# Strassen products for the last ten inner tiles of the first FFN of a hybrid block

## The chip, the cores and the metric

The kernel runs on one core of a Trainium2 chip. The metric is the time of one execution on the device in microseconds (us). TensorE (PE) does the matrix products from weights and moving operands in SBUF into PSUM banks, VectorE (DVE) and ScalarE (ACT) the elementwise work, GpSimd (POOL) little; SyncE (SP) and POOL issue most of the transfers.

## The reference

One decoder block in fp32: a macaron of two SwiGLU FFNs round a pair of token mixers. D = 1024, 512 tokens and 16 meta tokens ahead of them (L = 528), inner width D_FF = 2816.

```python
h = concat([meta, x])                                    # 528 x 1024
h = h + 0.5 * swiglu_ffn(rms_norm(h, ffn1_norm), ffn1_w1, ffn1_w3, ffn1_w2)
u = rms_norm(h, mix_norm) @ w_in                         # conv, ssm and gate inputs
h = h + (g_conv * conv_branch(u) + g_ssm * s5_branch(u)) @ w_out
h = h + 0.5 * swiglu_ffn(rms_norm(h, ffn2_norm), ffn2_w1, ffn2_w3, ffn2_w2)
out = rms_norm(h)[:, 16:]

def swiglu_ffn(x, w1, w3, w2):
    return (silu(x @ w1) * (x @ w3)) @ w2
```

The tokens lie along the free axis; a tile of 128 rows holds 128 features. The change is in the first FFN, before which stands only the load of x.

## The kernel before

**Products of fp32.** Every operand is split into a high part, cast to fp32r by ACT (line 120), and a low part, the difference, by DVE (line 121). A product is three matmuls: high by high, weights' low by high, high by low (`mm3`, line 147).

**First FFN, up.** D_FF is 22 inner tiles of 128. For a tile f, `ffn_up` loads the 1024 x 128 pieces of `ffn1_w1` and `ffn1_w3` (each as one 128 x 1024 tile, 512 KB, by SP into `raw`), splits them (`whi`, `wlo`) and multiplies them with x: 8 steps k of the depth, 3 terms, two halves of 264 tokens, each half in a PSUM bank of its own (`two()`). The moving operands `xh[k]`, `xl[k]` (split x with the norm's gain) stay in SBUF. The norm's factor r comes in where DVE evicts the banks (line 217), then ACT takes silu, DVE multiplies (line 239, `take`) and splits the hidden tile.

**First FFN, down.** Tiles go in groups of 8, 7 and 7. Behind a group, `down` multiplies for each of the eight output tiles k all hidden tiles of the group with `ffn1_w2`, and DVE adds the two halves into the residual `h[k]` (line 564). In the last group each output tile is followed by the operand of the next stage and its sum of squares.

**Preparation of the SSM.** `prepare_ssm` is a generator of elementwise work on the SSM's parameters, independent of the tokens: exponentials, the matrices bm, the c matrices (`cm`, line 288, written out to DRAM as `cd`), and the e tables (lines 499 to 514). `prep_step()` runs one step at a lower priority (`LATER`), after tiles with f even or above 8.

**Second FFN.** It does its 512 tokens already by Strassen pairs: `moving` forms four combinations t1 to t4 of the quarters of x, `pair` takes two inner tiles by seven `product`s (line 932) in place of eight, from weight quarters and sums of quarters. A `quarter` with two indices is loaded by SP and the second one added by a DMA of POOL (line 900). Down projections are taken between the products.

**The order.** No order is written out by hand. The program issues operations as above; a scheduler of the tile framework orders each engine by priority, with its own model of when operands are ready. Pools of buffers bound how far ahead work can go: 6 PSUM banks for these products (`psp`), 4 raw tiles (`rawp`), 7 split weights (`wsp`), 4 temporaries (`tp`), 18 hidden tiles (`hid1`).

Of the kernel before, what the change touches and what calls it, by code (L numbers as in the profile page):

```python
# [15 lines left out]
P = 128  # L16
# [10 lines left out]
G = 32  # L27
# [9 lines left out]
TAPS = 500  # L37
MAGIC = float(1.5 * 2 ** 23)
# [3 lines left out]
def tile_hybrid_block(  # L42
    ctx: ExitStack, tc: tile.TileContext,
    xt, cols, lam, bt, ct, dt, ffn1_w1, ffn1_w3, ffn1_w2, w_in, conv_proj, w_v, w_g, w_out,
# [38 lines left out]
    def tmp2(tag="m", bufs=2):  # L83
        return mp.tile([P, L], F32, tag=tag, name=nm(tag), bufs=bufs)
# [5 lines left out]
    mp = tst.enter_context(tc.tile_pool(name="mp", bufs=2, side="right"))  # L90
    ones = mp.tile([P, P], F32, name="ones", bufs=1)
# [119 lines left out]

    def ffn_gate(pss, r, n, take):
# [42 lines left out]
    def prepare_ssm(prep):  # L255
# [228 lines left out]
        while m < C:  # L484
            t = prep.tile([P, 3, G], F32, name=f"turn{m}")
# [10 lines left out]
        for i in range(4):  # L496
# [4 lines left out]
            for j, t in enumerate(turn):  # L501
                m = 2 ** j
                n = min(m, C - m)
                w = prep.tile([P, 2, 8, n], F32, tag="tw", name=nm("tw"))
# [19 lines left out]
    with ExitStack() as st:  # L524
        hid = st.enter_context(tc.tile_pool(name="hid1", bufs=18))
        pst = st.enter_context(ExitStack())
        prep = pst.enter_context(tc.tile_pool(name="prep", bufs=1))
# [25 lines left out]
        ssm_steps = prepare_ssm(prep)  # L553
# [16 lines left out]

        f0 = 0
        for nf in (8, 7, 7):
            hd = Hidden(slot, L)
            for f in range(f0, f0 + nf):
                if f == 0:
                    ffn_gate(first, r, L, hd.take)
                else:
                    ffn_up(ffn1_w1, ffn1_w3, f, r, L, hd.take)
                if f % 2 == 0 or f > 8:
                    prep_step()  # L580
            for k in range(KD):
# [6 lines left out]
        for _ in ssm_steps:  # L588
            raise AssertionError
        pst.close()  # L590


    with ExitStack() as st:
        mx = st.enter_context(tc.tile_pool(name="mx", bufs=1))
        sps = st.enter_context(ExitStack())
# [274 lines left out]
    with ExitStack() as st:  # L870
# [12 lines left out]
        def wide(pool, tag):  # L883
            return pool.tile([P, 8 * P], F32, tag=tag, name=nm(tag))

        def w4(tile_):
            return tile_.rearrange("p (w k c) -> p w k c", w=2, k=4)

        def split_w(src):
            hi = wsp.tile([P, 8 * P], F32R, tag="w", name=nm("whi"))  # L890
            lo = wsp.tile([P, 8 * P], F32R, tag="w", name=nm("wlo"))
            split(hi, lo, src)
            return w4(hi), w4(lo)

        def quarter(p, q, add=None):

            t = wide(rawp, "raw") if add is None else wide(xp, "x")
            nc.sync.dma_start(t, ffn2_up[p, q])
            if add is not None:
                PL.dma_start(t, ffn2_up[p, add], accum_op=ALU.add)  # L900
            return t

# [43 lines left out]
        def pair(p, hd):  # L946

            r11, s1, s3, r12, r22 = (quarter(p, *q) for q in ((0,), (1, 3), (0, 1), (2,), (3,)))
# [37 lines left out]
        def plain(p, hd):  # L986

            for tile_ in range(2):
                pss = [one(), one()]
                for kh in range(2):  # L990
                    wh, wl = split_w(quarter(p, 2 * kh + tile_))
# [86 lines left out]
def layout(i):  # L1078
# [13 lines left out]
    def up(w1, w3):  # L1092
# [18 lines left out]
        "ffn1_w1": tiles(i["ffn1_w1"], P), "ffn1_w3": tiles(i["ffn1_w3"], P),  # L1111
# [28 lines left out]
```

## Time and profile before

| | us |
|---|---|
| median of 3 runs (1074.3 to 1076.5) | 1074.4 |
| the profiled execution | 1074.19 |
| its span, in the trace | 1072.4 |
| TensorE busy | 1058.8 |
| VectorE busy | 752.2 |
| ScalarE busy | 407.3 |
| GpSimd busy | 42.3 |

The profile is of one execution; the granted TensorE clock was 0.997 of full speed over it. In the page's picture of the span PE is busy for nine tenths and more in all slices but the first and the last. The first FFN ends, with the second normalisation, a little after 417 us; the second one starts its pairs at about 743 us.

### The profile page before, as it was taken

Reading aid. Unit: us, or ns where it says so; the run is one execution under the profiler, and the core shown is the slowest. Engines: PE = TensorE matmul, PEld = TensorE weight load, DVE = VectorE, ACT = ScalarE, POOL = GpSimd, SP = SyncE. Lnnn points to the kernel's source line nnn. Section 1 sums busy time; section 2 is a strip of 40 time slices with the busy share of each in tenths; the row PEclk is TensorE's granted clock in tenths of the full one; section 3 lists DMA queues with packets and bytes.
Section 4 is the critical chain, followed back from the end, with each engine's and each line's share of the span. In section 5 each row is a group of like instructions: output and inputs, shape, how many; then the busy total and the mean of one; then the engine's idle time right before and its main releaser. Section 6 shows DMA issues by size and latency. Waiting matters only on the chain.

```text
span 1072.4 us, 18043 instructions
## 1 busy us (share of the span) xinstructions
PE 1058.8 (99%) x7316; PEld 986.7 (92%) x7316; DVE 752.2 (70%) x1401; ACT 407.3 (38%) x528; POOL 42.3 (4%) x81
## 2 busy tenths in 40 slices
PE   8999999999999999999999999999999999999997
PEld 7999999999999999998888788888999999998896
DVE  7997397953334465889899668558967786686672
ACT  6223322322222243215555363446443343243333
POOL 0000000000000000001000000010000000000001
PEclk9999999999999999999999999999999999999999
DMA  7324364232232232465653223254664464655122
GB/s 248 117 96 104 129 184 173 94 102 91 99 99 79 82 98 98 120 189 153 183 157 119 79 79 118 97 173 112 184 172 126 133 180 128 182 153 153 59 79 79
DMA packets 63267, 136.74 MB, mean 128 GB/s; under 512 B 22352, under 2 KB 29008, under 8 KB 63184
## 3 DMA queue, kind: packets, MB, share of 16 engines
q1 hardware_dynamic: 54192, 111.79, 32.7%
q0 software_dynamic: 4800, 16.78, 7.6%
q10 hardware_dynamic: 4192, 7.02, 2.1%
q8 instruction: 57, 0.93, 0.3%
q14 instruction: 26, 0.21, 0.1%
HBM read 124.50 MB, written 11.01 MB: 126 GB/s over the span
## 4 chain that ended last, share of the span: by engine, by line
PE 96%; DVE 1%; DMA 1%; ACT 1%; issue 0%; POOLq 0%; POOL 0%; SPq 0%; DVEq 0%; ACTq 0%
PE pp L147 62%; PE pp L932 17%; PE pm L1010 9%; PE pp L995 2%; PE pp L1064 2%; PE pm L455 1%; PE pm L649 1%; PE pm L684 1%; PE pm L685 1%; DMA raw<-in_ffn_w_dram 0%; DVE wlo L121 0%; DMA raw<-in_ffn_rows_dram 0%; PE pm L180 0%; DMA h<-in_x_dram 0%; PE pm L193 0%; DVE tl L121 0%
## 5 line engine op out<-in xcount | busy, mean ns | idle before, releaser
L121 DVE TENSOR_TENSOR wlo<-raw,whi 128x1024 fp32r<-128x1024 f32 (+2 forms) x177 | 207.5, 1174 | 185.4 <-issue 98.0
L120 ACT CAST whi<-raw 128x1024 fp32r<-128x1024 f32 (+2 forms) x177 | 178.2, 1011 | 396.7 <-PE pp L147 269.3
L147 PE MATMUL pp<-xh,whi 128*128 128x264 f32 (+1 forms) x1024 | 236.3, 301 | 1.6 <-DVE t L217 1.5
L147 PE MATMUL pp<-xl,whi 128*128 128x264 f32 (+1 forms) x1024 | 235.1, 301 | 2.6 <-DVE xl L154 2.6
L147 PE MATMUL pp<-xh,wlo 128*128 128x264 f32 (+1 forms) x1024 | 236.8, 301 | 0.0
L147 PEld LDWEIGHTS pp<-xh,whi 128*128 128x128 f32 x1024 | 165.0, 189 | 8.6 <-issue 1.5
L147 PEld LDWEIGHTS pp<-xl,whi 128*128 128x128 f32 x1024 | 163.6, 189 | 8.7 <-DVE xl L154 2.8
L147 PEld LDWEIGHTS pp<-xh,wlo 128*128 128x128 f32 x1024 | 164.5, 189 | 5.8
L147 PE MATMUL pp<-hd,whi 128*128 128x264 f32 x704 | 116.3, 285 | 0.0
L147 PEld LDWEIGHTS pp<-hd,whi 128*128 128x128 f32 x704 | 98.0, 189 | 0.0
L1010 PE MATMUL pm<-hd,whi 128*128 128x512 f32 x288 | 94.9, 395 | 0.0
L932 PE MATMUL pp<-th,whi 128*128 128x256 f32 x320 | 89.7, 282 | 0.8 <-ACT th L120 0.8
L932 PE MATMUL pp<-th,wlo 128*128 128x256 f32 x320 | 90.0, 282 | 0.2 <-DVE wlo L121 0.2
L932 PE MATMUL pp<-tl,whi 128*128 128x256 f32 x320 | 89.6, 282 | 0.3 <-DVE tl L121 0.3
L726 DVE SCALAR_TENSOR_TENSOR acc<-z,col,acc 128x512 f32<-128x512 f32 x120 | 84.8, 745 | 1.8 <-ACT acc L724 1.4
L147 PE MATMUL pp<-hd,wlo 128*128 128x264 f32 x352 | 72.6, 286 | 0.0
L932 PE MATMUL pp<-xh,whi 128*128 128x256 f32 x240 | 67.4, 281 | 0.0
L932 PE MATMUL pp<-xl,whi 128*128 128x256 f32 x240 | 67.3, 281 | 0.0
L932 PE MATMUL pp<-xh,wlo 128*128 128x256 f32 x240 | 67.3, 280 | 0.0
L1010 PEld LDWEIGHTS pm<-hd,whi 128*128 128x128 f32 x288 | 54.1, 188 | 11.3
L932 PEld LDWEIGHTS pp<-th,whi 128*128 128x128 f32 x320 | 60.1, 188 | 2.0 <-ACT th L120 1.0
L932 PEld LDWEIGHTS pp<-th,wlo 128*128 128x128 f32 x320 | 60.2, 188 | 1.4 <-DVE wlo L121 0.4
(279 smaller groups left out, 1619.2 us busy)
## 6 DMA issues: line engine op xcount, KB each, us to landing
raw<-in_ffn_w_dram SPq DMA_DIRECT2D x50, 512.0 KB, 3.5
raw<-in_ffn_up_dram SPq DMA_DIRECT2D x34, 512.0 KB, 4.4
raw<-in_w_in_dram SPq DMA_DIRECT2D x28, 512.0 KB, 3.6
x<-in_ffn_up_dram SPq DMA_DIRECT2D x20, 512.0 KB, 3.9
x<-in_ffn_up_dram POOLq DMA_DIRECT2D x20, 512.0 KB, 7.2
rd<-in_ffn_w_dram SPq DMA_DIRECT2D x24, 384.0 KB, 4.0
raw<-in_ffn_w_dram SPq DMA_DIRECT2D x16, 448.0 KB, 3.2
raw<-in_w_out_dram SPq DMA_DIRECT2D x8, 512.0 KB, 3.6
```

The lines of the kernel that those rows point to most:

```text
L120: A.copy(hi, src)
L121: V.tensor_tensor(lo, src, hi.bitcast(F32), op=ALU.subtract)
L147: nc.tensor.matmul(o, a[:, k, off:off + P], mov(k, n, lo), start=(k == 0 and j == 0), stop=(k == nk - 1 and j == 2))
L455: nc.tensor.matmul(ps[:, g, :], xm[(g0 + g) // Q][:, (g0 + g) % Q].rearrange("p l h -> p (l h)"), t[:, g, :], start=True, stop=True)
L649: nc.tensor.matmul(pb[j][:, g * C:(g + 1) * C], bm[:, g * P:(g + 1) * P], ub[i][:, j * 4 + g, :], start=True, stop=True)
L684: nc.tensor.matmul(o, tm[:, gs_], ub[i][:, j * 4 + g, CM:], start=True, stop=False)
L685: nc.tensor.matmul(o, cm[:, gs_], sa[i][:, j * 4 + g, CM:C], start=False, stop=True)
L726: V.scalar_tensor_tensor(o, src, w, o, op0=ALU.mult, op1=ALU.add)
L932: nc.tensor.matmul(ps[:, i * N2:(i + 1) * N2], a[:, i, k], b(k, lo), start=(first and i == 0 and k == 0 and j == 0), stop=(i == 1 and k == ...
L995: nc.tensor.matmul(pss[i], a[:, i, k], x[k + 4 * kh][:, :S], start=(kh == 0 and k == 0 and j == 0), stop=(kh == 1 and k == 3 and j == 2))
L1010: nc.tensor.matmul(ps, a[:, q * P:(q + 1) * P], hd.hl[q][lo], start=(q == 0 and j == 0), stop=(q == nf - 1 and j == 2))
L1064: nc.tensor.matmul(ps, a[:, tk], wts[q][b][j], start=False, stop=(q == nf - 1 and jj == 2))
```

## The change

`NP1 = 12`: inner tiles 0 to 11 are computed as before, in groups of 6 and 6. Tiles 12 to 21 become five pairs by Strassen products, in groups of 4 and 6 tiles, whose weights come packed by quarters (`ffn1_up`). A pair works on the two halves of 264 tokens; every product has two results (`w1` and `w3`) and takes two PSUM banks (`two()`).

- `moving(k)` stands after every second down projection of the second group. It loads x again, scales it, forms t1 to t4 and splits them; t1 takes the place of the second half of `xh[k]`, `xl[k]` for k below 4, and t2 to t4 get tiles of their own.
- The down projections of the group of 4 are taken one after each of the seven products of the next group's first pair and the eighth after the first product of its second pair; those of the last group stand at the end.
- The steps of the preparation come after tiles 0, 2, 4 (two), 6, 7 and 8 and after the first down projection. Its pool is closed after tile 11, and its room goes to `sp1`, the buffers of the pairs. The pool `turns` (powers for the e tables) moves to the other side, and the mixers' temporaries `m` get a pool that opens after the FFN.
- `hid1` has 14 tiles in place of 18. `wide`, `w4`, `split_w` and `quarter` move out of the second FFN, unchanged but for their buffers.

```diff
+NP1 = 12
...
-        hid = st.enter_context(tc.tile_pool(name="hid1", bufs=18))
+        hid = st.enter_context(tc.tile_pool(name="hid1", bufs=14))
...
+        def again(k):
+            raw = rawp.tile([P, 8 * P], F32, tag="raw", name=nm("raw"))[:, :L]
+            nc.sync.dma_start(raw, xt[k * P:(k + 1) * P, :])
+            t = tmp()
+            A.activation(t, raw, AF.Copy, scale=g1[:, k:k + 1])
+            return t
+
+        def moving(k):
+            xa, xb = again(k), again(k + 4)
+            t = sp1.tile([P, 4, HALF], F32, tag=f"c{k % 2}", name=nm("c"))
+            V.tensor_tensor(t[:, 0], xa[:, i1], xa[:, i0], op=ALU.subtract)
+            V.tensor_tensor(t[:, 1], xb[:, i1], t[:, 0], op=ALU.subtract)
+            V.tensor_tensor(t[:, 2], xa[:, i1], xb[:, i1], op=ALU.subtract)
+            V.tensor_tensor(t[:, 3], xb[:, i0], t[:, 1], op=ALU.subtract)
+            split(xh[k][:, i1], xl[k][:, i1], t[:, 0])
+            tw = [sp1.tile([P, 3, HALF], F32R, name=f"tw{q}{k}") for q in "hl"]
+            split(*tw, t[:, 1:])
+            tws.append(tw)
...
+        def product(pss, w, name, first=True):
+            b = b_of(name)
+            for i, ps in enumerate(pss):
+                for k in range(4):
+                    for j, (a, lo) in enumerate(((w[0], 0), (w[1], 0), (w[0], 1))):
+                        nc.tensor.matmul(ps, a[:, i, k], b(k, lo),
+                                         start=(first and k == 0 and j == 0),
+                                         stop=(k == 3 and j == 2), skip_group_check=not first)
+
+        def pair(p, hd):
+            r11, s1, s3, r12, r22 = (quarter(ffn1_up, sp1, p, *q)
+                                     for q in ((0,), (1, 3), (0, 1), (2,), (3,)))
+            ca, cb = (sp1.tile([P, 2, L], F32, tag=f"c{q}", name=nm("c")) for q in range(2))
+            t1, t2 = v2h(tmp()), v2h(tmp())
...
+            b1 = two()
+            product(b1, split_w(r11), "11")
+            for i in range(2):
+                A.copy(t1[:, i], b1[i])
+            yield
+            V.tensor_tensor(r11, r11, s1, op=ALU.add)
+            b6 = two()
+            product(b6, split_w(r11), "t2")
+            each(t1, b6, t1, ALU.subtract)
+            yield
+            b5 = two()
+            product(b5, split_w(s1), "t1")
+            each(t2, b5, t1, ALU.add)
+            yield
+            b7 = two()
+            product(b7, split_w(s3), "t3")
+            each(cb[:, :, i1], b7, t2, ALU.add)
+            yield
+            product(b1, split_w(r12), "21", first=False)
+            each(ca[:, :, i0], b1, r[:, i0], ALU.mult)
+            V.tensor_tensor(r12, r12, r11, op=ALU.add)
+            yield
+            b3 = two()
+            product(b3, split_w(r12), "22")
+            each(ca[:, :, i1], b3, t2, ALU.subtract)
...
+            product(b7, split_w(r22), "t4", first=False)
+            each(cb[:, :, i0], b7, t1, ALU.add)
...
-        for nf in (8, 7, 7):
+        for nf in (6, 6):
...
-                if f % 2 == 0 or f > 8:
+                if f in (0, 2, 4, 6, 7, 8):
                     prep_step()
+                if f == 4:
+                    prep_step()
...
             for k in range(KD):
                 down(f0, nf, hd, k)
-                if f0 + nf == NF:
-                    operand(k, hv[k], g2[:, k:k + 1], L)
-                    ssn.add(hv[k], V)
+                if f0 == 0 and k == 0:
+                    prep_step()
+                if f0 and k % 2:
+                    moving(k // 2)
             f0 += nf
+        hd = None
+        for nf in (4, 6):
+            old, hd = hd, Hidden(slot, L)
+            todo = [] if old is None else [(f0 - 4, 4, old, k) for k in range(KD)]
+            for p in range((f0 - NP1) // 2, (f0 + nf - NP1) // 2):
+                for _ in pair(p, hd):
+                    if todo:
+                        down(*todo.pop(0))
+            f0 += nf
+        for k in range(KD):
+            down(f0 - 6, 6, hd, k)
+            operand(k, hv[k], g2[:, k:k + 1], L)
+            ssn.add(hv[k], V)
```

DVE in a tile of the third group before: `wlo` is a split weight, `pp` a PSUM bank, `t` the evicted results, `hd` a hidden tile.

```order
621 L121 TENSOR_TENSOR wlo_392_3936<-raw_390_3934,whi_391_3935 128x1024
622 L217 TENSOR_TENSOR t_381_3866<-pp_374_3760,r_24_337 128x264
623 L217 TENSOR_TENSOR t_381_3866<-pp_375_3761,r_24_337 128x264
624 L121 TENSOR_TENSOR wlo_401_4004<-raw_399_4002,whi_400_4003 128x1024
625 L217 TENSOR_TENSOR t_382_3867<-pp_379_3816,r_24_337 128x264
626 L217 TENSOR_TENSOR t_382_3867<-pp_380_3817,r_24_337 128x264
627 L239 TENSOR_TENSOR t_382_3867<-t_382_3867,t_381_3866 128x528
628 L121 TENSOR_TENSOR hd_384_3875<-t_382_3867,hd_383_3874 128x528
```

DVE in the first pair of the changed kernel, from its second product's split on; line 650 evicts, line 672 adds quarters, `x` is a quarter with another added by POOL's DMA.

```order
612 L124 TENSOR_TENSOR wlo_359_3314<-x_337_3203,whi_358_3313 128x1024
613 L650 TENSOR_TENSOR t_342_3212<-pp_348_3247,t_342_3212 128x264
614 L124 TENSOR_TENSOR wlo_361_3344<-raw_338_3206,whi_360_3343 128x1024
615 L650 TENSOR_TENSOR t_342_3212<-pp_349_3248,t_342_3212 128x264
616 L672 TENSOR_TENSOR raw_338_3206<-raw_338_3206,raw_335_3198 128x1024
617 L650 TENSOR_TENSOR t_343_3213<-pp_352_3279,t_342_3212 128x264
618 L650 TENSOR_TENSOR t_343_3213<-pp_353_3280,t_342_3212 128x264
619 L124 TENSOR_TENSOR wlo_365_3377<-raw_338_3206,whi_364_3376 128x1024
620 L650 TENSOR_TENSOR c_341_3211<-pp_356_3311,t_343_3213 128x264
621 L124 TENSOR_TENSOR wlo_369_3414<-raw_339_3208,whi_368_3413 128x1024
622 L650 TENSOR_TENSOR c_341_3211<-pp_357_3312,t_343_3213 128x264
623 L650 TENSOR_TENSOR c_340_3210<-pp_344_3214,r_24_340 128x264
```

Where a split stood once to two evictions that follow each other, splits and evictions now alternate, and an addition of quarters stands ahead of the two evictions of the third product.

DVE before, round the first e table (`e0`), which stands among the down projections of the first group, behind the last c matrix `cm3`.

```order
402 L564 SCALAR_TENSOR_TENSOR h6_104<-pp_184_1967,h6_104 128x264
403 L288 TENSOR_TENSOR cm0_2201<-bt1_795,bt2_796 128x8x16
404 L564 SCALAR_TENSOR_TENSOR h6_104<-pp_185_1968,h6_104 128x264
405 L288 TENSOR_TENSOR cm1_2202<-bt1_795,bt2_796 128x8x16
406 L288 TENSOR_TENSOR cm2_2203<-bt1_795,bt2_796 128x8x16
407 L288 TENSOR_TENSOR cm3_2204<-bt1_795,bt2_796 128x8x16
408 L499 MEMSET e0_2414 128x8
409 L500 MEMSET e0_2414 128x8
410 L121 TENSOR_TENSOR wlo_207_2259<-raw_205_2257,whi_206_2258 128x1024
411 L564 SCALAR_TENSOR_TENSOR h7_105<-pp_189_2025,h7_105 128x264
```

The same place in the changed kernel; line 241 evicts a tile's result, line 263 is its gate product.

```order
396 L312 TENSOR_TENSOR cm2_1416<-bt1_798,bt2_799 128x8x16
397 L312 TENSOR_TENSOR cm3_1417<-bt1_798,bt2_799 128x8x16
398 L124 TENSOR_TENSOR wlo_221_2255<-raw_219_2253,whi_220_2254 128x1024
399 L241 TENSOR_TENSOR t_174_1905<-pp_171_1854,r_24_340 128x264
400 L241 TENSOR_TENSOR t_174_1905<-pp_172_1855,r_24_340 128x264
401 L523 MEMSET e0_1949 128x8
402 L524 MEMSET e0_1949 128x8
403 L263 TENSOR_TENSOR t_174_1905<-t_174_1905,t_173_1904 128x528
404 L534 TENSOR_TENSOR tw_177_1952<-e0_1949,turn1_1916 128x8
405 L535 TENSOR_TENSOR tw_177_1952<-e0_1949,turn1_1916 128x8
```

The first e table now stands among the tiles of the second group, ahead of a gate product.

## Rows read from the trace of the kernel before

**Rows 1.** The page, part 1: busy us of each engine, share, instructions.

```profile
PE 1058.8 (99%) x7316; PEld 986.7 (92%) x7316; DVE 752.2 (70%) x1401; ACT 407.3 (38%) x528; POOL 42.3 (4%) x81
```

**Rows 2.** The page, part 4: the chain that ended last, by engine and by line.

```profile
PE 96%; DVE 1%; DMA 1%; ACT 1%; issue 0%; POOLq 0%; POOL 0%; SPq 0%; DVEq 0%; ACTq 0%
PE pp L147 62%; PE pp L932 17%; PE pm L1010 9%; PE pp L995 2%; PE pp L1064 2%; PE pm L455 1%; PE pm L649 1%; PE pm L684 1%; PE pm L685 1%; DMA raw<-in_ffn_w_dram 0%; DVE wlo L121 0%; DMA raw<-in_ffn_rows_dram 0%; PE pm L180 0%; DMA h<-in_x_dram 0%; PE pm L193 0%; DVE tl L121 0%
```

**Rows 3.** The chain in order of time: start us, us, what.

```profile
135.65 281.36 PE pp L147 x2304
...
743.03 36.06 PE pp L932 x302
```

**Rows 4.** Waits of PE: line, waited for: us in total, times, longest.

```profile
PE pp L147 <- DVE xl L154: 2.6, 1, 2.6
...
PE pp L932 <- ACT th L120: 0.8, 1, 0.8
...
PE pp L932 <- DVE tl L121: 0.3, 1, 0.3
PE pp L932 <- DVE wlo L121: 0.2, 1, 0.2
```

**Rows 5.** Stretches: us, busy PE, PEld, DVE, ACT, POOL (instructions), PEclk, DMA, GB/s.

```profile
165.00:232.00 67.00, 67.00 (x549) 67.00 (x549) 55.03 (x194) 18.64 (x23) 2.02 (x5) 1.00 0.36 117
...
764.00:784.00 20.00, 20.00 (x159) 19.46 (x158) 18.15 (x23) 9.29 (x12) 1.73 (x2) 1.00 0.71 201
...
940.00:966.00 26.00, 26.00 (x219) 25.91 (x218) 23.30 (x27) 12.82 (x17) 1.74 (x2) 1.00 0.59 158
```

**Rows 6.** Groups by shape: count, busy us, mean ns, idle time before.

```profile
L121 DVE TENSOR_TENSOR wlo<-raw,whi 128x1024 fp32r<-128x1024 f32 x153 | 186.7, 1223 | 142.4 <-issue 69.5 <-PE pp L147 50.8 <-PE pp L932 10.5
L120 ACT CAST whi<-raw 128x1024 fp32r<-128x1024 f32 x153 | 160.0, 1050 | 344.2 <-PE pp L147 225.5 <-PE pm L1010 27.4 <-DVE raw L955 26.0
L217 DVE TENSOR_TENSOR t<-pp,r 128x264 f32<-128x264 f32 x88 | 33.9, 424 | 0.1
L121 DVE TENSOR_TENSOR wlo<-rd,whi 128x768 fp32r<-128x768 f32 x24 | 23.0, 957 | 17.3 <-issue 13.8 <-PE pp L932 3.5
L239 DVE TENSOR_TENSOR t<-t,t 128x528 f32<-128x528 f32 x22 | 15.5, 704 | 1.2
L981 DVE TENSOR_TENSOR c<-c,r 128x1024 f32<-128x1024 f32 x10 | 12.2, 1218 | 0.0
```

**Rows 7.** DVE in time: start, us, what; x2 is two back to back.

```profile
749.02 2.35 DVE L121 TENSOR_TENSOR wlo<-raw,whi 128x1024 fp32r<-128x1024 f32 x2
...
253.50 0.77 DVE L564 SCALAR_TENSOR_TENSOR h<-pp,h 128x264 f32<-128x264 f32 x2
...
81.85 0.69 DVE L121 TENSOR_TENSOR hd<-t,hd 128x528 fp32r<-128x528 f32 x1
82.47 0.48 DVE L288 TENSOR_TENSOR xm<-bt,bt 128x128 f32<-128x128 f32 x2
```

**Rows 8.** Loads of weight quarters; POOL's issues in ns; landing of the accumulating ones.

```profile
x<-in_ffn_up_dram SPq DMA_DIRECT2D x20, 512.0 KB, 3.9
...
L900 POOL DMA_DIRECT2D x<-in_ffn_up_dram x20: 863/872/942, 714.1 to 985.3; - x20
...
DMA to landing us min/median/max: 5.2/7.2/8.6
```

**Rows 9.** DVE groups from 137 to 232 us, as in rows 6.

```profile
L513 DVE TENSOR_TENSOR e<-e,turn 128x16 f32<-128x16 f32 (+5 forms) x56 | 10.4, 230 | 0.0
...
L511 DVE TENSOR_TENSOR tw<-e,turn 128x16 f32<-128x16 f32 (+5 forms) x28 | 6.4, 228 | 0.0
L288 DVE TENSOR_TENSOR cm<-bt,bt 128x128 f32<-128x128 f32 x28 | 6.3, 284 | 0.2
...
L288 DVE TENSOR_TENSOR bt<-s_ai,q 128x512 f32<-128x512 f32 x6 | 4.1, 689 | 0.1
```

**Rows 10.** DVE in time, as in rows 7, at the first e table.

```profile
165.51 0.07 DVE L499 MEMSET e<- 128x8 f32 x1 [4.78 <-DMA cd<-cm]
```

More of the change, by code (lines that the diff above doesn't have):

```diff
@@ L83, in tmp2 @@
     def tmp2(tag="m", bufs=2):
-        return mp.tile([P, L], F32, tag=tag, name=nm(tag), bufs=bufs)
+        pool = mmp[0] if tag == "m" else mp
+        return pool.tile([P, L], F32, tag=tag, name=nm(tag), bufs=bufs)
     ident = cst.tile([P, P], F32, name="ident")
@@ L209, in movx, with wide, w4, split_w @@
         return (xl if lo else xh)[k].rearrange("p (t c) -> p t c", t=T)[:, :, CM:]
+    def wide(pool, tag):
+        return pool.tile([P, 8 * P], F32, tag=tag, name=nm(tag))
+    def w4(tile_):
+        return tile_.rearrange("p (w k c) -> p w k c", w=2, k=4)
+    def split_w(src):
+        hi = wsp.tile([P, 8 * P], F32R, tag="w", name=nm("whi"))
+        lo = wsp.tile([P, 8 * P], F32R, tag="w", name=nm("wlo"))
+        split(hi, lo, src)
+        return w4(hi), w4(lo)
+    def quarter(up, xp, p, q, add=None):
+        t = wide(rawp, "raw") if add is None else \
+            xp.tile([P, 8 * P], F32, tag="x", name=nm("x"), bufs=2)
+        nc.sync.dma_start(t, up[p, q])
+        if add is not None:
+            PL.dma_start(t, up[p, add], accum_op=ALU.add)
+        return t
     def ffn_gate(pss, r, n, take):
@@ L484, in prepare_ssm @@
         while m < C:
-            t = prep.tile([P, 3, G], F32, name=f"turn{m}")
+            t = turns.tile([P, 3, G], F32, name=f"turn{m}")
             if not turn:
@@ new lines, in pair, with each @@
+        def pair(p, hd):
[3 more added lines that the diff above has]
+            t1, t2 = v2h(tmp()), v2h(tmp())
+            def each(o, a, b, op):
+                for i in range(2):
+                    V.tensor_tensor(o[:, i], a[i], b[:, i] if len(b.shape) == 3 else b, op=op)
+            b1 = two()
+            product(b1, split_w(r11), "11")
+            for i in range(2):
+                A.copy(t1[:, i], b1[i])
[20 more added lines that the diff above has]
+            each(ca[:, :, i1], b3, t2, ALU.subtract)
+            V.tensor_tensor(ca[:, :, i1], ca[:, :, i1],
+                            r[:, i1].unsqueeze(1).to_broadcast([P, 2, HALF]), op=ALU.mult)
+            A.activation(ca[:, 0], ca[:, 0], AF.Silu)
+            hd.take(ca[:, 1], ca[:, 0])
+            yield
+            product(b7, split_w(r22), "t4", first=False)
+            each(cb[:, :, i0], b7, t1, ALU.add)
+            V.tensor_tensor(cb, cb, r.unsqueeze(1).to_broadcast([P, 2, L]), op=ALU.mult)
+            A.activation(cb[:, 0], cb[:, 0], AF.Silu)
+            hd.take(cb[:, 1], cb[:, 0])
+            yield
@@ L881, in slot @@
             return hid.tile([P, S], F32R, tag="hd", name=nm("hd"))
[L883 to L901, printed above, removed]
         th = [thp.tile([P, 4, N2], F32R, name=f"th{k}") for k in range(4)]
@@ L946, in pair @@
         def pair(p, hd):
-            r11, s1, s3, r12, r22 = (quarter(p, *q) for q in ((0,), (1, 3), (0, 1), (2,), (3,)))
+            r11, s1, s3, r12, r22 = (quarter(ffn2_up, xp, p, *q) for q in ((0,), (1, 3), (0, 1), (2,), (3,)))
             ca, cb = c2(), c2()
```

38 lines of the change are left out of this document (29 added, 9 removed).

## The prediction

> **What bounds the kernel now.** I read the totals of the engines first, then the chain of waits, then the waits of TensorE alone, then engine time by stretches. TensorE (PE) is busy for 1058.8 of 1072.4 us [rows 1], and 96% of the chain that ended last is its own work, 62% of it in the matmuls of the helper at line 147 [rows 2], which the first FFN uses. From 135.65 us the chain is one piece of 281.36 us and 2304 matmuls, hence 0.1221 us from one 264-column matmul to the next [rows 3]. Over the whole run the waits of PE for other engines come to 7.2 us in 7 lines, from 2.6 us downwards; the three of line 932, 1.3 us together, lie where the second FFN enters its Strassen pairs [rows 4]. So in the first FFN time is a count of matmuls times 0.1221 us, as long as every operand is ready. The vector engine (DVE) has room there: even while the last steps of the SSM preparation run beside the tiles it is busy for 55.03 of 67 us, and PE for all 67 [rows 5].
>
> **The change part by part.** *Matmuls.* Tiles 12 to 21 cost 10 tiles x 2 weights x 8 k x 3 terms x 2 halves = 960 matmuls of 264 columns. Five pairs cost 5 x 7 products x 2 weights x 4 k x 3 terms = 840. The moving operand is still 264 columns wide and each matmul still has its own weight load, so I take the same pitch: 120 x 0.1221 = 14.7 us less. That the pitch holds in the Strassen form is seen in the second FFN, where 302 matmuls of 256 columns take 36.06 us, 0.1194 each, with no wait between them [rows 3]. The down projection in groups of 6, 6, 4, 6 has as many matmuls as in 8, 7, 7: each (tile, output row, term, half) once.
>
> *DVE in a pair.* It has 7 weight splits and 2 quarter additions of 1024 columns, 12 evictions of 264, one product with r of 1056 and one of 528, two gate products and two hidden splits of 528. By single durations [rows 6]: 7 x 1.223 + 3 x 1.218 (the 1024 row for 1056 too) + 12 x 0.424 + 5 x 0.704 = 20.8 us. By what one adds behind another (two splits 2.35, so 1.13 more; two evictions 0.77, so 0.34; a 528 instruction starts 0.62 before the next) [rows 7]: 10 x 1.13 + 12 x 0.34 + 5 x 0.62 = 18.5 us. PE needs 168 x 0.1221 = 20.5 us for the pair. The nearest thing measured is the second FFN's pair: 18.15 us of DVE in 20 us (0.91), with PE busy for all 20, and with a down projection between the products 23.30 in 26 us, PE again busy throughout [rows 5]. I take the second sum, as it is the one that a queue pays: 18.5 of 20.5, the share (0.90) that did not hold PE back there. In the one pair with a down projection between its products DVE has more room, since a down of 4 tiles is 24 matmuls, 2.9 us, for a split of 512 columns and two evictions, about 1.3 us.
>
> *Order inside a pair.* From the start of the first product DVE has the last down's evictions (0.7 us), then the rows shown in the section on the change: split, eviction (not before the first half of the second product ends, 4.4 us), split, eviction (5.9), addition, two evictions (7.3 and 8.8), split. Added up at the queue's pitch that last split, for the sixth product, ends at about 10.3 us; PE needs it at 5 x 2.93 = 14.7 us. The same sum carried to the second pair leaves 3 to 4 us everywhere. ACT has 7 x 1.05 us of casts and six short instructions, half of the 20.5 us. No term.
>
> *Loads with addition.* Per pair two quarters are loaded (median 3.9 us) and a second one is added by a DMA from POOL (5.2 to 8.6 us) [rows 8]: 12.5 us at worst from the moment the buffer is free. By the sum above the first is free about 1.4 us before the pair starts and wanted by the addition at about 15.0 us: 3.9 us to spare. Nothing.
>
> *Entry into the pairs.* Four calls of the moving-operand helper stand between the down projections of the second group: per call 4 subtractions and a split of 264 and one split of 792 columns, about 5 x 0.34 + 0.87 (0.957 for 768 columns [rows 6], less the 0.09 that the queue saves on a wide split) = 2.6 us of DVE, 10.3 us for four, beside 8 x (0.87 + 0.68) = 12.4 us of downs, in 35 us of PE. It reads x again from DRAM and waits for no result of the downs, unlike the same step in the second FFN, which cost 1.3 us of PE [rows 4]. Between 0 and 1.3 us; I take 1.3, the measured one.
>
> *Preparation moved forward.* No DVE or PE instruction is added; the steps end within 12 tiles instead of 11, but without the down group that stood among them. From the first down group to the end of tile 11 DVE then has 8 downs of 1.55 and 6 tiles of 4.9 (two splits 2.26, four evictions 1.36, a gate product and a hidden split 1.24), 42 us of FFN work, and about 47 us of preparation (the c matrices 15.2 in three lines, the e tables 32.0 in four, of each the largest and the smallest shown [rows 9]), in 288 + 6 x 96 = 864 matmuls, 105 us of PE. That is a share of 0.85, between 55.03 of 67 (0.82) and the 0.91 of the second FFN's pair, neither of which cost anything [rows 5]. The wait of the first e table for the write of the c matrix (4.78 us [rows 10]) now falls among the tiles: DVE stands before tile 6's gate product, while PE has three half tiles, 17 us, of split weights before it. Bounds 0 and 4.8 us; I take 0. SP's extra issues (x again, more but smaller weights) wait for buffers as the old ones did.
>
> *After the FFN.* From the second normalisation on the order on PE is the one of before. Nothing.
>
> The sum: 1074.19 us of the profiled execution (1.8 us round its span) - 14.7 + 1.3 = **1060.8 us**; that execution is 0.2 us under the median shown, which changes nothing.
>
> **The rivals.** *Vector-bound pairs.* Four of the five pairs run almost without downs. If DVE pays single durations, 20.8 against 20.5 us loses 4 x 0.3 = 1.2 us; if each of their 28 products waits for one eviction of 0.34 us, 9.5 us. That gives 1062 to 1070, middle 1066. For it: two evictions of 264 instead of one of 512 per product. Against it: the shares above.
>
> *PSUM banks, on the slower side.* A product now holds two of the six banks; from the fourth product on, two more pairs of banks are held for results that accumulate later, so two remain. If PE must wait at every product until the two evictions of the one before are through, 35 x 0.68 = 23.8 us are lost: 1074.2 - 14.7 + 23.8 = 1083. It decides from 0.42 us a product (14.7 / 35), and is slower by more than noise from 0.48. Against it: a product lasts 2.9 us, and the order lets an eviction stand only one split (1.13 us) back.
>
> *Late additions.* Each pair's first addition could hold the whole vector queue. If an accumulating DMA took twice its median of 7.2 us, 3.9 + 14.4 = 18.3 us against 16.4 would stop each of four pairs for 1.9 us: 1068. Against it: POOL's issue took 863 to 942 ns in the second FFN, at most 0.08 us longer than its shortest, beside a DVE that was nine tenths busy [rows 5, 8]. The Trainium skill (SBUF — State Buffer, Who interferes with whom) says that VectorE and GpSimd share a pair of SBUF ports, held by one of them for a whole instruction, and that GpSimd writes the descriptors of the DMAs it issues through it. By that rule an issue could be put off by a whole vector instruction each time; the trace does not show it, and the page itself doubts it for tensor-tensor instructions, which these are.
>
> That the change does not do what it says is excluded: the order on PE has the 840 matmuls.
>
> **How the numbers follow.** Forecast 0.64 (1059 to 1062.5), vector-bound pairs 0.23, late additions 0.05, banks 0.08. No change means within 0.2%, 2.1 us, about what a measurement of this kernel can tell. Of the second and third case 0.03 may end there, the banks are slower, the rest faster: 0.89, 0.03, 0.08. The range runs from 1058.5 (no wait at all, and a run's scatter of 1 us) to 1070.5, the end of the vector-bound case; it leaves out the banks and a little of the late additions.
>
> **What would show it.** In the new profile the product line has 840 matmuls at 0.122 us, and PE has under 2 us of waits between the first normalisation and the second; the second normalisation starts 13 to 15 us earlier. Vector-bound pairs would show as many short waits of PE for the whi, wlo splits in the two stretches of pairs without downs; banks as waits of the product line for evictions (t, c) of line 650 in all pairs; late additions as a DVE wait for the DMA into x. More than 17 us of PE idle in the first FFN makes the forecast wrong in sign.

## The result, and the profile after

The changed kernel takes 1060.18 us (median of 4 runs, 1059.03 to 1060.84), the kernel before 1074.91 beside it: a ratio of 0.9858, with a 95% interval of 0.9845 to 0.9871, or 14.7 us less. Forecast were 1060.8 us, faster. A second set of runs of the same kernel later gave 0.9860 (0.9844 to 0.9876).

The page of the changed kernel, parts 1 and 4, answers to [rows 1, 2].

```profile
PE 1042.4 (98%) x7196; PEld 971.1 (92%) x7196; DVE 813.3 (77%) x1504; ACT 434.7 (41%) x577; POOL 50.7 (5%) x91
...
PE 95%; DMA 2%; DVE 1%; ACT 1%; issue 0%; POOLq 0%; POOL 0%; DVEq 0%; ACTq 0%
```

PE has 120 instructions and 16.4 us of work less, DVE 61 us more, and PE still bounds. The chain in order of time (start us, us, what) answers to [rows 3].

```profile
112.69 121.75 PE pp L150 x997
234.44 43.82 PE pp L637 x360
...
322.11 37.98 PE pp L637 x312
360.09 41.83 PE pp L150 x344
...
460.12 5.73 DMA tm<-td
...
1014.28 4.61 DMA raw<-in_ffn_rows_dram
```

From 112.69 us to 401.92, where the sums of the second normalisation stand, the chain is PE alone: the products (line 637) follow the tiles without a gap. Before, that point came at 417.01 us (135.65 + 281.36 [rows 3]), so the first FFN gave back 15.1 us. A matmul of the pairs takes 43.82 / 360 = 0.1217 us, one before 0.1221.

The waits of PE, in us, count and longest, answer to [rows 4].

```profile
PE pp L150 <- DVE xl L157: 2.9, 1, 2.9
PE pp L150 <- DVE t L241: 1.5, 1, 1.5
...
PE pm L822 <- DMA tm<-td: 0.8, 1, 0.8
```

Line 637 is not among them. Those of xl and t lie before 33 us, in both kernels. The one for `tm`, in the SSM, is new. Stretches (us; busy PE, PEld, DVE, ACT, POOL; PEclk, DMA, GB/s) answer to [rows 5]: tiles with the last of the preparation, the entry, the first pair, the second pair with a product of the third, the third pair with the eight downs of the group of 4, the fourth pair, and all pairs together.

```profile
112.70:165.00 52.30, 52.30 (x430) 52.30 (x430) 46.45 (x150) 13.87 (x16) 1.98 (x2) 1.00 0.78 230
...
202.00:234.40 32.40, 32.40 (x269) 32.40 (x267) 23.79 (x47) 14.75 (x21) 0.00 (x0) 1.00 0.47 150
234.44:254.90 20.46, 20.46 (x171) 20.46 (x170) 16.04 (x24) 8.36 (x10) 1.72 (x2) 1.00 0.68 181
254.90:278.30 23.40, 23.40 (x194) 23.40 (x194) 20.56 (x30) 10.10 (x14) 1.72 (x2) 1.00 0.58 158
278.30:322.10 43.80, 43.80 (x362) 43.80 (x361) 33.71 (x55) 18.52 (x27) 1.72 (x2) 1.00 0.47 133
322.10:342.50 20.40, 20.40 (x171) 20.40 (x170) 17.46 (x26) 8.71 (x10) 1.73 (x2) 1.00 0.64 173
...
234.44:360.09 125.65, 125.65 (x1035) 125.65 (x1034) 102.66 (x155) 53.05 (x70) 6.88 (x8) 1.00 0.54 147
```

PE is busy for the whole of each, at the full clock; DVE for 0.73 to 0.89.

### The profile page after: what moved, and what is told of

Read it like the earlier page. It is cut to its first block, busy times and chain, and to the rows that moved or that the text cites. A ratio compares the mean times of both kernels' runs of the same rounds, so it can differ in the third digit from the quotient of the medians.

```text
span 1059.0 us, 18082 instructions
## 1 busy us (share of the span) xinstructions
PE 1042.4 (98%) x7196; PEld 971.1 (92%) x7196; DVE 813.3 (77%) x1504; ACT 434.7 (41%) x577; POOL 50.7 (5%) x91
## 3 DMA queue, kind: packets, MB, share of 16 engines
q0 software_dynamic: 6240, 22.02, 10.3%
## 4 chain that ended last, share of the span: by engine, by line
PE 95%; DMA 2%; DVE 1%; ACT 1%; issue 0%; POOLq 0%; POOL 0%; DVEq 0%; ACTq 0%
PE pp L150 51%; PE pp L1050 18%; PE pp L637 10%; PE pm L1128 9%; PE pp L1113 2%; PE pp L1182 2%; PE pm L479 1%; PE pm L787 1%; PE pm L822 1%; PE pm L823 1%; DMA tm<-td 1%; DMA pb<-in_b_dram 1%; DVE wlo L124 0%; DMA raw<-in_ffn_rows_dram 0%; PE pm L183 0%; DMA raw<-in_ffn_w_dram 0%
## 5 line engine op out<-in xcount | busy, mean ns | idle before, releaser
L123 ACT CAST whi<-raw 128x1024 fp32r<-128x1024 f32 (+3 forms) x190 | 184.2, 977 | 353.5 <-PE pp L150 163.8
L124 DVE TENSOR_TENSOR wlo<-raw,whi 128x1024 fp32r<-128x1024 f32 (+3 forms) x190 | 215.0, 1133 | 116.6 <-PE pp L150 42.3
L150 PE MATMUL pp<-xl,whi 128*128 128x264 f32 (+1 forms) x704 | 170.1, 308 | 2.9 <-DVE xl L157 2.9
L150 PE MATMUL pp<-xh,whi 128*128 128x264 f32 (+1 forms) x704 | 170.6, 308 | 2.3 <-DVE t L241 1.5
L150 PE MATMUL pp<-xh,wlo 128*128 128x264 f32 (+1 forms) x704 | 171.2, 309 | 0.0
L150 PEld LDWEIGHTS pp<-xh,whi 128*128 128x128 f32 x704 | 114.8, 189 | 8.9 <-issue 1.5
L150 PEld LDWEIGHTS pp<-xl,whi 128*128 128x128 f32 x704 | 114.2, 190 | 9.0 <-DVE xl L157 3.2
L150 PEld LDWEIGHTS pp<-xh,wlo 128*128 128x128 f32 x704 | 114.5, 189 | 5.8
L150 PE MATMUL pp<-hd,whi 128*128 128x264 f32 x704 | 119.0, 285 | 0.0
L150 PE MATMUL pp<-hd,wlo 128*128 128x264 f32 x352 | 74.8, 286 | 0.0
```

The costliest lines, as they stand in the source:

```text
L123: A.copy(hi, src)
L124: V.tensor_tensor(lo, src, hi.bitcast(F32), op=ALU.subtract)
L150: nc.tensor.matmul(o, a[:, k, off:off + P], mov(k, n, lo), start=(k == 0 and j == 0), stop=(k == nk - 1 and j == 2))
```

## The experiments

Each kernel was timed beside the kernel before. Times are medians; "the end of the first FFN" is where the sums of the second normalisation start on PE (401.76 us after, 416.85 before; the chain above counts from the end of the instruction ahead of them). That stretch begins somewhat earlier or later from execution to execution, so "the length of the first FFN" is counted from the end of the wait for `t`, which every kernel here has at about 31 us: 383.98 us before (from 32.87), 368.88 us after (from 32.88).

A "late start" is a matmul that starts more than 0.3 us after the one ahead of it. Its loss is that distance less 0.122 us. It is about 0.16 us more than the wait that the list of waits shows, because a matmul counts as busy for 0.28 us there, while the next one can start 0.122 us after it. The sums of late starts below are counted from the starts in the traces.

### Only the groups and the preparation: plain_tail

```diff
-                if f0 and k % 2:
-                    moving(k // 2)
...
         for nf in (4, 6):
...
+            hd = Hidden(slot, L)
+            for f in range(f0, f0 + nf):
+                ffn_up(ffn1_w1, ffn1_w3, f, r, L, hd.take)
...
```

> Groups of 6, 6, 4, 6 and the preparation moved forward as in the changed kernel, but tiles 12 to 21 as plain tiles: no pairs, no second reading of x. Count theory (the gain is 120 matmuls at 0.122 us, and nothing else of the change is seen in the time): 1074.9 us, as before, and 14.6 us above the changed kernel. Rival, regrouping: part of the gain comes from the other groups and the earlier preparation, since fewer matmuls of the preparation or waits stand in the first FFN; then 1073 or less, 2 us and more under before. Rival, hidden price: the preparation on a shorter stretch costs up to the 4.8 us of the e table's wait; then 1077 to 1080.

1074.54 us, 0.9991 of before (0.9981 to 1.0). The end of the first FFN (start us, us):

```profile
416.48 1.08 PE L183 MATMUL pm<-ones,sqa 128*128 128x1 f32 x10
```

Between 30 and 420 us PE has one wait, the 1.5 us for `t` that every kernel here has.

The first FFN takes 384.02 us (from 32.46), before 383.98. The count theory holds: the regrouping and the earlier preparation are worth nothing and cost nothing that shows in it. The pairs alone make the gain.

### Three pairs: three_pairs

```diff
-NP1 = 12
+NP1 = 16
-        for nf in (6, 6):
+        for nf in (6, 6, 4):
...
-        for nf in (4, 6):
+        for nf in (6,):
```

> Groups of 6, 6, 4 plain tiles and one group of three pairs. Count theory with no price for the entry: 72 matmuls fewer than before, 8.8 us, so 1066.1 us, 5.9 above the changed kernel; one pair is worth 2.93 us. Rival, entry: the pairs gain more than the count says and the entry costs 1.3 us as in the second FFN; by 15.1 us measured at the end of the first FFN, (15.1 + 1.3) / 5 = 3.3 us a pair, then 1074.9 - 9.8 + 1.3 = 1066.4, which the total hardly tells apart, but the profile does: PE would wait near the first product.

1066.69 us, a ratio of 0.9919 (0.9905 to 0.9934), against 0.9858 with five pairs. The difference is 6.5 us for two pairs, where the count says 5.9; the total does not tell the two apart. The profile does: it has one wait near the first products, 0.3 us for the high half of a weight, a late start of 0.4 us. The first FFN takes 375.51 us (33.48 to 408.99), 8.5 less than before, where the count says 8.8. So the entry costs 0.4 us here, not 1.3.

### The operands formed late: late_moving

```diff
-                if f0 and k % 2:
-                    moving(k // 2)
+                if f0 and k == KD - 1:
+                    for q in range(4):
+                        moving(q)
```

> The four calls that form the operands of the pairs stand together behind the eighth down projection of the second group, not one after every second. Spread theory (the entry costs nothing because the 10 us of DVE work lie between the downs): the second product needs the combination t2 of all four calls, 2.9 us after the last down; DVE needs some 10 us from when they may start, so PE stops for 3 to 7 us, 1063 to 1067 us. Rival, readiness: the calls read only x and the norm's gain, so that the scheduler takes them early all the same, and the place in the program does not matter: 1060.2 us.

1060.76 us, 0.9861 (0.9844 to 0.9877): the spread theory is wrong, the rival right in the time. The last operands on DVE (start us, us):

```profile
233.93 0.42 DVE L617 TENSOR_TENSOR c<-t,c 128x264 f32<-128x264 f32 x1
235.52 0.98 DVE L124 TENSOR_TENSOR twl<-c,twh 128x792 fp32r<-128x792 f32 x1
```

In the changed kernel the last of these splits starts at 220.62 us. Here it ends at 236.50, PE turns to the product that reads it at 236.99, and nothing waits. The calls are ready from their loads on, so the scheduler takes them among the downs although they stand behind them: the first of their subtractions starts at 212.24 us, and the downs run on PE until 234.06. But it does not take them as early as in the changed kernel, where that subtraction starts at 200.76. So the place in the program does matter; it ate up all but about 0.5 us of the lead, and a little more would have shown in the time.

### More work for DVE in the pairs: dve_264 and dve_1024

Behind every product one more addition on a buffer `dum`, of 264 or of 1024 columns, whose result is not used.

```diff
+            V.tensor_tensor(dum, dum, dum, op=ALU.add)
```

> One more DVE addition of 264 columns behind every product of the pairs (on a buffer of its own, the result is not used): 7 x 0.34 = 2.4 us a pair by what one adds in the queue. Cover theory (DVE has 16 to 17.5 us of work in the 20.5 us of a pair): 18.4 to 19.9 of 20.5, still hidden, 1060.2 to 1061 us. Rival, latency: a product already stands close behind the eviction or the split it needs, and each 0.34 us on the queue shows: 35 x 0.34 = 11.9, 1072 us.

1060.68 us, 0.987 (0.9853 to 0.9886), so hidden. But the dose was not the one meant: the additions wait for nothing, and the scheduler put about 20 of the 35 ahead of the pairs, and the last one at 252.5 us. That makes one stretch, the first pair, the sharper test:

```profile
233.90:257.00 23.10, 23.10 (x192) 23.10 (x191) 22.96 (x42) 9.73 (x12) 1.72 (x2) 1.00 0.60 160
```

DVE is busy for 22.96 of 23.10 us, and PE still for all of them. A full DVE does not stop PE as long as the splits made ahead last. What the additions cost came behind that stretch, in two late starts at 283 and 285 us: the first FFN takes 369.47 us (from 32.25), 0.6 more than in the changed kernel.

> One more DVE addition of 1024 columns behind every product of the pairs (on a buffer of its own): 7 x 1.13 = 7.9 us a pair. Cover theory: 16 to 17.5 + 7.9 = 24 to 25.4 us of DVE against 20.5 of PE, so DVE sets the pace: 3.5 to 5 us a pair, 17 to 25 us in five, 1077 to 1085 us; the waits of PE are for the low halves of the weights. Rival, banks: the first thing to run out are the PSUM banks, and the waits of PE are for evictions into t and c; then a similar time with another releaser.

1074.12 us, 0.9994 (0.9985 to 1.0004): 14 us lost, in the direction expected and under the range. Again the additions moved forward, the last one is at 319.9 us, so the last two pairs had none. The stretch that held 26 of them, and the same length from the start of the pairs in the changed kernel:

```profile
233.00:320.00 87.00, 79.36 (x603) 75.72 (x603) 85.09 (x115) 30.71 (x41) 5.15 (x6) 0.98 0.51 137
```

```profile
234.30:321.30 87.00, 87.00 (x717) 87.00 (x716) 69.72 (x106) 36.97 (x50) 5.15 (x6) 1.00 0.55 152
```

26 additions of 1.13 us are 29 us on top of 69.7, together 99 in 87: by this estimate 12 too much, and PE did 114 matmuls fewer, 13.9 us. The waits of PE in the list come to 7.3 us, for the splits (2.5), for evictions into c and t (2.0) and for downs and hidden tiles (2.8), so neither splits nor banks went first alone. Counted by the starts, that is 17 late starts, 10.6 of the 13.7 us by which the first FFN is longer; the rest are mostly matmuls right behind them or at a low clock (0.54 to 0.61 from 276 to 280 us).

### The transfers: no_add and one_x

In no_add the accumulating DMAs of the first FFN are left out, so that s1 and s3 hold one quarter each. one_x has one buffer for them.

```diff
-        if add is not None:
+        if add is not None and up is not ffn1_up:
```

> The accumulating DMAs of POOL in the first FFN are left out, so s1 and s3 hold one quarter instead of a sum. Theory (loads with addition are hidden and do not disturb DVE): 1060.2 us, within 0.2%. Rival, shared port or late additions: an issue on POOL delays DVE or a DVE addition waits for the transfer; then 1 to 2 us less.

1059.74 us, 0.9857 (0.9842 to 0.9872), the ratio of the changed kernel: POOL's ten DMAs cost neither DVE nor PE anything that can be measured.

```diff
-            xp.tile([P, 8 * P], F32, tag="x", name=nm("x"), bufs=2)
+            xp.tile([P, 8 * P], F32, tag="x", name=nm("x"), bufs=1 if up is ffn1_up else 2)
```

> One buffer instead of two for the summed quarters s1 and s3 of the pairs. s3 is then loaded only when the split of s1 is through, and s1 of the next pair only behind the split of s3. Load theory: load 3.6 and accumulate 7.2 us after that, plus cast and split 2.3, 13 us from one product's split to the next but one's; a product lasts 2.93 us and about 3.5 us of lead are there, so PE stops about 13 - 2.9 - 3.5 = 6 to 7 us for s3; for s1 of the next pair there is time from the fourth product to its first addition, 14 us, no stop. Five pairs: 30 to 35 us, 1090 to 1096 us. Rival, late addition is not the chain: under 10 us.

1092.86 us, 1.0163 (1.0147 to 1.0178): 32.7 us above the changed kernel, as expected, though not by the parts expected. The waits of PE in the pairs, and PE in the time round one of them:

```profile
PE pp L637 <- ACT whi L123: 18.6, 6, 4.3
```

```profile
243.00:245.00 2.00, 0.00 (x0) 1.00 0.16 29
245.00:247.00 2.00, 1.41 (x7) 0.88 0.00 0
247.00:249.00 2.00, 2.00 (x11) 0.50 0.77 248
...
251.00:253.00 2.00, 2.00 (x19) 1.00 0.86 193
```

The waits of the list are 19 us, not 30 to 35. PE stops until 245.15 us, starts again, and from 247 on runs at a granted clock of 0.50, which is 1.2 GHz: 11 matmuls begin or end in 2 us where 19 do at 2.4 GHz. In the order of time (start us, us, idle before):

```profile
242.12 0.28 PE L637 MATMUL pp<-xl,whi 128*128 128x264 f32 x1
245.15 0.51 PE L637 MATMUL pp<-twh,whi 128*128 128x264 f32 x2 [2.75 <-ACT whi L123]
...
247.16 0.42 PE L637 MATMUL pp<-twh,wlo 128*128 128x264 f32 x1
247.38 0.42 PE L637 MATMUL pp<-twl,whi 128*128 128x264 f32 x1
```

From start to start that stop is 3.03 us, and at the low clock the pitch is 0.22 us. Over the first FFN, which is 33.2 us longer than in the changed kernel, 19 late starts lose 24.2 us, and 89 matmuls more than there follow at 0.2 to 0.3 us, nearly all at the low clock, another 8.7. So the expected total was met by luck: the stops cost 24 us, not 30 to 35, and the expectation had no term for the clock.

### One pair more: six_pairs, six_late_e, six_46, and seven

```diff
-NP1 = 12
+NP1 = 10
...
-        hid = st.enter_context(tc.tile_pool(name="hid1", bufs=14))
+        hid = st.enter_context(tc.tile_pool(name="hid1", bufs=16))
...
-        for nf in (6, 6):
+        for nf in (6, 4):
...
-        for nf in (4, 6):
+        for nf in (6, 6):
```

> One pair more: groups of 6 and 4 plain tiles, then 6 and 6 as pairs, with 16 hidden tiles. Count theory: 24 matmuls fewer, 2.93 us, so 1057.3 us. Rival, preparation: its last steps have 10 tiles in place of 12 and the operand of the pairs comes 23 us earlier; where DVE, 46.5 of 52.3 us busy at that place in the changed kernel, has no room left, PE waits 3 us and more and the time stays at 1060 or above.

1071.69 us, 0.9965 (0.9952 to 0.9978), 11.5 above the changed kernel: the rival is right in the direction, and the price is higher than it said. PE round the entry (us, busy, PEclk):

```profile
196.00:202.00 6.00, 5.19 (x43) 1.00 0.87 264
202.00:206.00 4.00, 0.55 (x2) 0.82 1.01 305
206.00:210.00 4.00, 3.55 (x17) 0.50 1.05 265
210.00:215.00 5.00, 2.76 (x14) 0.84 0.48 122
215.00:220.00 5.00, 5.00 (x31) 0.68 0.42 141
```

The same stretch by engine, where DVE has no hole over 0.6 us but one of 2.7 us, ahead of the first addition of quarters:

```profile
184.50:214.50 30.00, 22.81 (x161) 21.68 (x159) 26.56 (x67) 12.29 (x20) 1.98 (x2) 0.89 0.69 195
```

DVE still makes e tables between 180 and 197 us, and only then the first operand. But PE's longest wait there does not end with DVE's queue. The first pair's loads of `x` wait for the last table, while in the changed kernel they start behind the writes of the c matrices. First the changed kernel's issue, then SyncE's wait in six_pairs (us, count, longest), the issues, and the cast, the matmul and the addition that they lead to (start us, us):

```profile
141.01 2.40 SPq L231 DMA_DIRECT2D x<-in_ffn_up_dram  x2
```

```profile
SPq L231 <- DVE e L538: 1.3, 1, 1.3
...
196.82 0.80 SPq L231 DMA_DIRECT2D x<-in_ffn_up_dram  x2
198.43 5.19 SPq L231 DMA_DIRECT2D raw<-in_ffn_up_dram  x4
204.35 1.04 ACT L123 CAST whi<-raw 128x1024 fp32r<-128x1024 f32 x1 [1.09 <-DMA raw<-in_ffn_up_dram]
205.45 0.81 PE L637 MATMUL pp<-xh,whi 128*128 128x264 f32 x2 [4.26 <-ACT whi L123]
210.77 1.23 DVE L657 TENSOR_TENSOR raw<-raw,x 128x1024 f32<-128x1024 f32 x1 [2.74 <-issue]
```

The cast waits for a load that SyncE issues behind those of `x`. DVE stands idle for 2.74 us ahead of the addition, which needs the accumulating DMA of 201.23 us. So two things hang on the tables here: DVE's queue, and the loads. What put the loads behind them is not shown; this kernel also has two more hidden tiles. In dve_264 they start as late, at 195.48 us, and cost nothing, since its pairs start at 233.80.

The waits of PE at the entry are 7 us in the list, and the low clock behind them adds to that. By the starts the first FFN, 379.83 us (from 32.86), is 13.9 longer than the count says: seven late starts lose 8.7 us and the matmuls at the low clock about 5, of which some 1.5 are older, since in this execution the clock was at 0.50 from 34 to 36 us too.

Two kernels took the tables out of the way, and with `hid1` back at 14 tiles: the preparation's pool closes behind the c matrices, and the tables are made at low priority beside the pairs (`prep_step()` after pairs 0 and 2), with two downs behind each of the first two products.

```diff
+        tust = st.enter_context(ExitStack())
-        turns = pst.enter_context(tc.tile_pool(name="turns", bufs=1, side="right"))
+        turns = tust.enter_context(tc.tile_pool(name="turns", bufs=1, side="right"))
...
-                if f in (0, 2, 4, 6, 7, 8):
+                if f in (0, 2, 4):
...
+                if p in (0, 2):
+                    prep_step()
```

> Six pairs as in the run of six pairs (plain tiles in groups of 6 and 4, pairs in groups of 6 and 6), but the e tables, 32 us of DVE work that needs only the small pool of powers, no longer stand ahead of the pairs: the preparation's pool closes behind the c matrices, and the tables come at low priority beside the pairs and the last down projections. 14 hidden tiles, and two downs after each of the first two products. Room theory (the run of six pairs lost 14 us because DVE was late into the pairs, with the e tables in front of the operands and the first splits): the entry costs nothing again and the sixth pair gives its 2.93 us: 1057.3 us (1056 to 1059). Rival, entry by itself: downs of 4 tiles (23 us of PE) are too short for the four calls that form the operands, whatever stands ahead; then PE waits 5 us and more at the entry and the time is 1063 or above. Rival, pairs full: the tables crowd the pairs, whose DVE is busy 16 to 17.5 of 20.5 us, and cost 5 to 10 us there: 1062 to 1067.

1062.34 us, 0.9872 (0.9854 to 0.9889): the first FFN takes 369.93 us (from 32.47), 9.9 less than in six_pairs and still 4.0 more than by the count. The room theory is right in its direction and its number is missed; the time falls into the range of the second rival, but not by its mechanism: of the waits of PE, 1.4 us for a down and 0.9 for a cast lie at the entry, where DVE was busy for 14.45 of 15 us (185 to 200), and 0.6 us in the pairs. So the place at which the downs are short is a part of it, as the first rival had it, at a smaller price. The run does not tell DVE's room from the loads: the first loads of `x` start at 140.58 us again, so both were put right at once.

> Seven pairs: plain tiles in groups of 4 and 4, pairs in groups of 4, 4 and 6, the e tables late as in the other kernel. Room theory: two pairs more than the changed kernel, 2 x 2.93 us: 1054.3 us, if the c matrices are written by the time the operands are formed; they end at about 165 us in the changed kernel, where its first plain tiles and downs leave DVE room, and here the entry comes at about 150 us, so that 0 to 8 us may be lost: 1054 to 1062. Rival, pairs full: as in the other kernel, 1060 to 1066.

1082.73 us, 1.0062 (1.0047 to 1.0077): slower than before. One wait of PE is 9.8 us long. From 112 to 150 us DVE has room, and then not:

```profile
112.00:150.00 38.00, 38.00 (x313) 38.00 (x312) 21.62 (x58) 13.60 (x31) 0.00 (x0) 1.00 0.47 123
150.00:181.00 31.00, 17.05 (x123) 16.29 (x121) 25.52 (x92) 11.42 (x19) 1.98 (x2) 0.84 0.81 274
```

So it is not the amount of DVE work. The last group of c matrices starts at 166.60 us, in the changed kernel at 137.73 (not 165, as the expectation had it). The matmuls of the step ahead of it (line 479), for which DVE waits, run from 115.3 to 137.4 us, in the changed kernel from 90.6 to 112.4. That fits the order of the program, which has the two steps after tile 4 behind eight downs of 4 tiles here (23 us of PE) and ahead of the downs there. The writes of the c matrices are issued from 166.9 us on, the first loads of `x` at 170.46, which fits buffers that take the place of that preparation.

```diff
-        for nf in (6, 4):   # of six_late_e; preparation after tiles 0, 2, 4 (two)
+        for nf in (4, 6):   # preparation after tiles 0, 1, 2, 3
```

> As the run of six pairs with late e tables (1062.3 us), but the plain tiles in groups of 4 and 6, so that the entry lies beside eight downs of 6 tiles, 35 us of PE, in place of eight of 4, 23 us; the five early steps of the preparation come after tiles 0 to 3 and the first down. Spread theory (what was lost there, 3 to 4 us, is lost because 12 us of downs and 10 us of operands fill DVE for 23 us: 22.6 of 25, 14.5 of 15 and 19.7 of 20 us busy): 1057.3 to 1059 us, under the changed kernel. Rival, amount: the work of DVE before the entry is the same and the room too, only its place differs; then the c matrices end later and the loss stays, 1061 to 1064 us.

> The changed kernel itself once more, beside the run of six pairs with longer downs, for a comparison on one chip: a ratio of 0.986 to before. By the count theory its first FFN ends within 0.3 us of where it ended in its first profile (401.9 us), while the wait of TensorE for the matrices tm, 0.8 us there, and the last transfers may come out otherwise, as chance of the transfers.

six_46 took 1059.71 us, 0.9861 (0.9846 to 0.9876), after_again 1059.75, 0.9860: the same. The spread theory is right for the entry, where no wait is left, but the sixth pair's 2.9 us still do not appear. The end of the first FFN of the two:

```profile
401.41 1.08 PE L183 MATMUL pm<-ones,sqa 128*128 128x1 f32 x10
```

```profile
402.60 1.08 PE L183 MATMUL pm<-ones,sqa 128*128 128x1 f32 x10
```

Counted from the end of the wait for `t` (32.41 us in six_46, 32.88 in the changed kernel's first profile), the FFN takes 369.0 us, with five pairs 368.9, and by the count it should be 365.9. The 3.0 us missing are five late starts, 2.6 us, and the matmuls right behind them, which start about 0.1 us late each. The largest, 1.0 us, is in the downs of the first group, where DVE takes a step of the preparation ahead of an eviction; three lie where two downs of six tiles follow a product of the pairs (start us, us, idle before):

```profile
267.64 0.51 PE L150 MATMUL pp<-hd,whi 128*128 128x264 f32 x2 [0.23 <-ACT whi L123]
268.63 0.51 PE L150 MATMUL pp<-hd,wlo 128*128 128x264 f32 x2 [0.48 <-DVE wlo L124]
```

So this kernel moved the loss from the entry to other places. No kernel here beats the changed one clearly.

## Why the prediction was right

- **Matmuls.** 14.7 us forecast, 15.1 found in the first FFN, and plain_tail shows that they come from the pairs alone. The 0.4 us on top are mostly the shorter pitch: 840 x (0.1221 - 0.1217) = 0.3 us.
- **DVE in a pair.** The queue's sum, 18.5 us a pair and 1.3 a down, makes 5 x 18.5 + 8 x 1.3 = 102.9 us; measured are 102.66 in the 125.65 us of the pairs. That they agree so closely is luck, since some of the first pair's instructions ran ahead of that window and some of the next downs' are in it. For the 155 in it the queue's sum is about 99 us and that of single durations 111, so the measured time lies between, nearer to the queue's. The vector-bound rival fell not by the sum but by the waits, of which line 637 has none, and the two doses show how far: PE keeps going through one pair with DVE at 0.99, and loses what is too much when DVE is overfilled for longer.
- **Order in a pair.** Forecast was the sixth product's split at 10.3 us after the start. In the first pair, which starts at 234.28, it ends at 245.38, 11.1 us after, where PE needs it at 14.7. (The rows for that order begin with the split of the fourth product's weights, not of the second's, which had started at 230.32, ahead of the pair; the forecast's sum is not changed by it.)

```profile
244.15 1.23 DVE L124 TENSOR_TENSOR wlo<-raw,whi 128x1024 fp32r<-128x1024 f32 x1 [0.48 <-ACT whi L123]
```

- **Loads with addition.** No wait, and no_add shows no price. The issue on POOL and the landing were, against [rows 8]:

```profile
L233 POOL DMA_DIRECT2D x<-in_ffn_up_dram x30: 854/863/1139, 148.0 to 970.0; - x30
...
DMA to landing us min/median/max: 5.2/7.2/10.0
```

Two issues, those of the first pair at 148 us, were 0.21 and 0.28 us longer than the shortest, the others at most 0.07: not whole vector instructions each time. The cover is one buffer thick: one_x.
- **Entry into the pairs.** This is the term that was mis-sized: 1.3 us were taken from the second FFN, and 0 were paid. The prediction's own reason against it, that the calls wait for no result of the downs, was the right one; late_moving bears it out, with about 0.5 us to spare.
- **Preparation.** 0 was right; the wait for the c matrix's write [rows 10] is gone from DVE's waits. six_pairs shows how near the edge lies: with 35 us of PE less ahead of the entry (two tiles, and downs of 4 in place of 6) and the first pair's loads behind the last table, the first FFN ends 10.9 us later than with five pairs, not 2.9 earlier. That the pairs' loads can wait for the preparation's buffers was not in the prediction.
- **Banks.** No wait for an eviction in the pairs of the changed kernel. That a full set of banks would stop PE shows only in dve_1024, as 2.0 us.
- **After the FFN.** Forecast was nothing. The first profile lost 0.6 us between the first FFN and the last loads, where the wait of 0.8 us for `tm` is new, and 1.1 us from these loads on. That cancels the 1.7 us that the FFN gave beyond the sum, so that its time, 1060.84 us, met the 1060.8 by luck. after_again waits 0.7 us for `tm` too, no_add and dve_264 not at all. What sets that wait stays open; it is about as large as the scatter of the runs.

## What to carry to other kernels

Where PE is busy without a gap, the price of a change is its matmuls by their pitch, and everything else is a question of whether what feeds it keeps its lead: the vector queue, and the loads with the buffers that they need. Add that queue up by what one instruction adds behind another; single durations give too much, but where the queue has holes, the sum gives a little too little. A saving of this kind can end at once: the same step that gave about 3 us a pair up to five pairs gave nothing or a loss with the sixth. In two kernels the loss lay at the entry, where the vector engine's other work had lost its room and, in one of them, the first loads waited for that work's buffers; in the third it lay in late starts elsewhere. A term borrowed from a like place should be kept only if its cause is there too.

## What the runs showed of the hardware

A wait of PE can cost more than its length. Every kernel here has a wait of 1.5 us for `t` at about 31 us; the granted clock after it stayed at 1.00 in the changed kernel's first profile, but not in its second (us, PE busy, PEclk). It fell so in two of the 14 profiles, this one and that of six_pairs:

```profile
30.00:33.00 3.00, 1.54 (x12) 1.00 0.45 145
33.00:34.00 1.00, 1.00 (x10) 0.86 0.23 90
34.00:35.00 1.00, 1.00 (x6) 0.50 0.00 0
...
37.00:38.00 1.00, 1.00 (x10) 0.93 0.00 0
```

There the next 471 matmuls of the chain took 59.34 us in place of 57.83: 1.5 us more for the same wait, which is as much as the runs of one kernel scatter. In one_x 24 us of late starts became 33 us of time, with the clock at 0.92 over the pairs and the downs behind them.
